# Sliding windows of 8 x 8: the early load on ScalarE's queue left out, and the eight last stores made into two

## The chip, the cores and the metric

The kernel runs on one core of a Trainium2 chip. The metric is the device time of one execution in microseconds. Before the change it is 190.47 us, the median of three runs (190.44 to 190.74).

## The reference

For every image, every window of 8 x 8 pixels with a stride of 4 is copied out, all 64 channels of it. There are 15 x 15 windows, so each input pixel is copied about four times: 16.78 MB come in, and 58.98 MB go out. Nothing is computed; the work is moving bytes.

```python
# x: [16, 64, 64, 64] float32, window_size 8, stride 4
for i in range(15):
    for j in range(15):
        result[:, i, j] = x[:, :, 4*i : 4*i + 8, 4*j : 4*j + 8]
# result: [16, 15, 15, 64, 8, 8]
```

## The kernel before

**The input in SBUF.** The whole input lies in one tile `L` of 128 partitions. A partition holds one image, one half of the channels (`ch`, 32 channels) and one band of 16 rows (`q`, four bands). Partition number: 64 x `ch` + 4 x image + `q`. So 32 neighbouring partitions (`QP`) are eight images (a block `y`, two of them) of one channel half, with all bands.

**The loads.** `load` (L56, issue at L58) brings one `ch`, `y` and `q`: eight partitions, every fourth. For each of the eight pairs of `y` and `q` there are three loads. SyncE's queue brings channels 4 to 31 of the first channel half (896 KB), GpSimd's queue channels 0 to 3 of it (128 KB) and the second channel half (1024 KB). Ahead of the loop ScalarE's queue issues one more load (L106): the first eight channels of band 0 of the second channel half, for all sixteen images, so 16 partitions and 512 KB. GpSimd's two loads of band 0 of the second half start behind these channels and are 768 KB each.

**The windows.** Four output tiles `G` of 128 partitions take turns (`tile_`). One partition of such a tile holds one whole window of one image, 64 channels x 8 x 8, which is 16 KB and one contiguous row of the output. `part` (L181) fills a tile for one `y`, in four blocks of 32 partitions by two channel halves; `unit` fills a tile for all images, with copies on ScalarE (L148) and shuffles on VectorE (L151, L158, and L162 for ScalarE's share). Windows that cross from one band to the next take their lower rows from the next partition (L151). Each filled tile is written by one indirect DMA from GpSimd (`scatter`, L128), which looks up the output row of every partition; 29 of these go out in all. A tile is filled again once its scatter has completed. All scatters stand in GpSimd's queue behind the loads.

**The last column.** Windows in column j = 14 that lie in one band, for the first two row positions (`s` = 0 and 1), have tiles of their own (L218 to L230). Only 64 partitions (32 to 95) of the tile are filled: two blocks of 32 partitions (`y`) by two channel halves (`ch`), `ch` 0 on ScalarE and `ch` 1 on VectorE, so two blocks for each engine. Four plain stores of 16 rows each follow, one for each band `q`; those of `s` = 0 go out on SyncE's queue, those of `s` = 1 in turn on SyncE's and ScalarE's.

```python
for s in range(2):
    g = tile_()
    ...
    for q in range(HQ):
        free((nc.sync, nc.scalar)[s * q % 2].dma_start(out=o_q[q * NSLOT + s, j], ...))
```

What sets the order: each engine and each queue works in the order of the program, with waits on the data and on the tiles. GpSimd's queue uses eight completion semaphores in turn, so its ninth load waits for its first.

Of the kernel before, what the change touches and what calls it, by code (L numbers as in the profile page):

```python
# [10 lines left out]
def kernel(  # L11
# [7 lines left out]
    nc = tc.nc  # L19
    P = nc.NUM_PARTITIONS  # L20

    B, C, H, W = x.shape
    Bo, NH, NW, Co, WSo, WSo2 = out.shape
    WS = int(window_size)
    ST = int(stride)
# [5 lines left out]
    CH = 2  # L31
    HQ = P // (B * CH)
    CL = C // CH
    RB = H // HQ
    NSLOT = RB // ST
    NWIN = NH * NW
    CFREE = C * WS * WS
    HP = P // CH
    YB = 8
    NY = B // YB  # L40
    QP = YB * HQ
# [7 lines left out]
    L = lpool.tile([P, CL, RB, W], f32)  # L49
# [6 lines left out]
    def load(eng, ch, y, q, c0, c1):  # L56
        p0 = ch * HP + y * QP + q
        eng.dma_start(out=L[p0 : p0 + QP - HQ + 1 : HQ, c0:c1, :, :], in_=x_v[ch, y, q, :, c0:c1, :])  # L58
# [41 lines left out]
    mul(th, tc_, NW)  # L100
    tt(idx_lo, idx_lo, th, ALU.add)


    EC = 8
    x_b = x.rearrange("b (ch cl) (hq r) w -> ch hq b cl (r w)", ch=CH, hq=HQ)
    nc.scalar.dma_start(out=L[HP : HP + (B - 1) * HQ + 1 : HQ, 0:EC, :, :], in_=x_b[1, 0, :, 0:EC, :])  # L106

    for y in range(NY):
        for q in range(HQ):
            hw = y * HQ + q < HWP  # L110
            if hw:
                load(nc.sync, 0, y, q, SMALL, CL)
            load(nc.gpsimd, 0, y, q, 0, SMALL if hw else CL)
            load(nc.gpsimd, 1, y, q, EC if q == 0 else 0, CL)

    o_v = out.rearrange("b i j c r w -> (b i j) (c r w)")
    nxt = [min(p + 1, 31) for p in range(32)]
# [3 lines left out]
    o_q = out.rearrange("b i j c r w -> i j b (c r w)")  # L121

    def free(st):
        tc.declare_no_dep(st.ins, group="stores", reason="each store writes rows of its own")
        tc.add_to_no_dep_group("stores", st.ins)
# [27 lines left out]
    act, dve = nc.scalar.copy, nc.vector.tensor_copy  # L153
# [15 lines left out]
    def tile_():  # L169
        nonlocal at  # L170
        at += 1
        return G[(at - 1) % NG]
# [43 lines left out]


    j = NW - 1  # L218
    tile_()
    for s in range(2):  # L220
        g = tile_()
        cols = slice(j * ST, j * ST + WS)
        for y in range(NY):
            d = slice(QP + y * QP, QP + (y + 1) * QP)
            for ch, copy in enumerate((act, dve)):
                f = slice(ch * HP + y * QP, ch * HP + (y + 1) * QP)
                copy(out=g[d, ch * CL : (ch + 1) * CL, :, :], in_=L[f, :, s * ST : s * ST + WS, cols])  # L227
        g_q = g.rearrange("p c r w -> p (c r w)")
        for q in range(HQ):
            free((nc.sync, nc.scalar)[s * q % 2].dma_start(out=o_q[q * NSLOT + s, j], in_=g_q[QP + q : QP + q + (B - 1) * HQ + 1 : HQ]))  # L230


# [33 lines left out]
```

## Time and profile before

| What | Before |
|---|---|
| Median of three runs | 190.47 us |
| The profiled execution | 190.74 us |
| Its span | 189.0 us |
| VectorE busy | 142.5 us (75%) |
| ScalarE busy | 139.2 us (74%) |
| GpSimd busy | 46.9 us (25%) |
| DMA, mean over the span | 401 GB/s, 11044 packets |
| GpSimd's queue (q0) | 65.81 MB, 84.0% of the 16 engines' span |
| SyncE's queue (q1) | 8.91 MB, 12.0% |
| ScalarE's queue (q10) | 1.05 MB, 1.8% |

The profile is of one execution, which took 190.74 us; its span, from the first to the last record, is 189.0 us. A line of the 40 slices gives the busy share in tenths, a slice being 4.7 us long. A share of DMA is the mean over the 16 engines. It can stand a little above 1, because packets overlap. The names in the queue lines: q0 "software_dynamic" is what GpSimd issues, q1 what SyncE issues, q10 what ScalarE issues.

### The profile page before, as it was taken

How to read it: one execution, taken by the hardware profiler on the slowest of the kernel's cores; microseconds unless marked ns; L12 is line 12 of the kernel's file. 1: busy time of each engine (PE TensorE's matmuls, PEld its weight loads, DVE VectorE, ACT ScalarE, POOL GpSimd, SP SyncE). 2: the span in 40 equal slices, each digit the busy share in tenths (PEclk: the TensorE clock that was granted, in tenths of full speed). 3: DMA queues.
4: the chain of work that ended last, by engine and by line, in shares of the span. 5: the costliest groups of instructions: out<-in, count | busy, mean ns of one | idle time of the engine just before them, and what ended most of it. 6: DMA issues, size and time to landing. Idle time of an engine off the chain costs nothing.

```text
span 189.0 us, 557 instructions
## 1 busy us (share of the span) xinstructions
DVE 142.5 (75%) x200; ACT 139.2 (74%) x89; POOL 46.9 (25%) x50
## 2 busy tenths in 40 slices
DVE  4000009999697979799989999999999999997410
ACT  0000009998699999988889999999999999974740
POOL 7321212207217170522220222222222222223000
DMA  4999999999999999999999999999999999999993
GB/s 118 308 409 397 402 401 397 397 403 394 427 434 420 435 434 416 434 434 413 437 437 408 439 430 420 423 437 416 427 413 434 428 409 430 406 437 378 427 389 153
DMA packets 11044, 75.81 MB, mean 401 GB/s; under 512 B 3344, under 2 KB 3344, under 8 KB 7440
## 3 DMA queue, kind: packets, MB, share of 16 engines
q0 software_dynamic: 8784, 65.81, 84.0%
q1 hardware_dynamic: 2048, 8.91, 12.0%
q10 hardware_dynamic: 208, 1.05, 1.8%
q14 instruction: 4, 0.03, 0.0%
HBM read 16.78 MB, written 62.91 MB: 422 GB/s over the span
## 4 chain that ended last, share of the span: by engine, by line
DMA 66%; DVE 18%; issue 6%; ACT 3%; POOL 2%; DVEq 0%; ACTq 0%; PEldq 0%
DMA out_dram<-G,idx_hi 24%; DMA L<-in_x_dram 23%; DMA out_dram<-G,idx 13%; DVE G L158 10%; DMA out_dram<-G,idx_y 7%; DVE G L151 5%; DVE G L181 3%; ACT G L227 2%; POOL L L58 2%; ACT G L148 1%; DVE G L148 0%; DVEq L181 0%; POOL pi L69 0%; DVEq L158 0%; PEldq L261 0%
## 5 line engine op out<-in xcount | busy, mean ns | idle before, releaser
L148 ACT COPY G<-L 64x2048 f32<-64x2048 f32 x46 | 87.2, 1896 | 5.5 <-DMA out_dram<-G,idx 2.3
L181 DVE COPY G<-L 32x2048 f32<-32x2048 f32 x30 | 36.6, 1221 | 29.3 <-DMA L<-in_x_dram 26.7
L158 DVE STREAM_SHUFFLE G<-L 64x1024 f32<-64x1024 f32 (+3 forms) x40 | 55.7, 1392 | 1.3
L151 DVE STREAM_SHUFFLE G<-L 64x1024 f32<-64x1024 f32 x30 | 38.5, 1282 | 0.0
L181 ACT COPY G<-L 32x2048 f32<-32x2048 f32 x18 | 33.9, 1896 | 2.9 <-DMA L<-in_x_dram 2.3
L181 ACT ACT_TABLE_LOAD x1 | 1.3, 1283 | 28.3 <-DMA L<-in_x_dram 28.3
L58 POOL DMA_DIRECT2D L<-in_x_dram x16 | 10.9, 691 | 23.0 <-DMA L<-in_x_dram 22.5
L128 POOL DMA_INDIRECT out_dram<-G,idx_y x6 | 10.0, 1664 | 25.5 <-DVE G L181 24.5
L128 POOL DMA_INDIRECT out_dram<-G,idx x8 | 11.3, 1412 | 19.9 <-DVE G L158 6.5
L128 POOL DMA_INDIRECT out_dram<-G,idx_hi x8 | 7.7, 963 | 30.7 <-DVE G L151 23.1
L128 POOL DMA_INDIRECT out_dram<-G,idx_lo x7 | 6.7, 961 | 27.5 <-DVE G L151 19.1
L227 ACT COPY G<-L 32x2048 f32<-32x2048 f32 x4 | 7.6, 1896 | 5.1 <-DMA out_dram<-G,idx_lo 4.0
L162 ACT COPY G<-L 64x256 f32<-64x256 f32 (+1 forms) x20 | 9.1, 456 | 0.5
L227 DVE COPY G<-L 32x2048 f32<-32x2048 f32 x4 | 4.9, 1219 | 3.5 <-DMA out_dram<-G,idx_hi 2.4
L148 DVE COPY G<-L 64x2048 f32<-64x2048 f32 x6 | 7.3, 1222 | 0.2
L158 DVE LOAD_MASK_SELECT G<-L x40 | 0.4, 9 | 2.1 <-DMA out_dram<-G,idx_y 1.2
L72 DVE TENSOR_SCALAR tb<-pi 128x1 int32<-128x1 int32 x1 | 0.2, 153 | 1.0 <-POOL pi L69 1.0
L78 DVE TENSOR_TENSOR th<-tc,tq 128x1 int32<-128x1 int32 x2 | 0.3, 156 | 0.0
L75 DVE TENSOR_SCALAR th<-tc 128x1 int32<-128x1 int32 x2 | 0.3, 154 | 0.0
L69 POOL IOTA pi<- 128x1 int32 x1 | 0.1, 124 | 0.4 <-PEq L261 0.4
L151 DVE LOAD_MASK_SELECT G<-L x30 | 0.2, 7 | 0.0
L78 DVE CUSTOM_DVE_ANT_0 idx_lo<-tb,th 128x2 uint16<-128x2 uint16 x1 | 0.2, 159 | 0.0
(18 smaller groups left out, 2.6 us busy)
## 6 DMA issues: line engine op xcount, KB each, us to landing
L<-in_x_dram SPq DMA_DIRECT2D x8, 896.0 KB
L<-in_x_dram POOLq DMA_DIRECT2D x6, 1024.0 KB, 21.6
L<-in_x_dram POOLq DMA_DIRECT2D x2, 768.0 KB, 18.3
out_dram<-G SPq DMA_DIRECT2D x6, 256.0 KB
L<-in_x_dram POOLq DMA_DIRECT2D x8, 128.0 KB, 21.6
L<-in_x_dram ACTq DMA_DIRECT2D x1, 512.0 KB
out_dram<-G ACTq DMA_DIRECT2D x2, 256.0 KB
out_dram<-G,idx POOLq DMA_INDIRECT x8, 12.3
```

What stands on the lines that cost most here:

```text
L58: eng.dma_start(out=L[p0 : p0 + QP - HQ + 1 : HQ, c0:c1, :, :], in_=x_v[ch, y, q, :, c0:c1, :])
L69: nc.gpsimd.iota(pi[:, :], pattern=[[0, 1]], base=0, channel_multiplier=1)
L72: nc.vector.tensor_scalar(out=d[:, :], in0=pi[:, :], scalar1=shift, scalar2=mask, op0=ALU.logical_shift_right, op1=ALU.bitwise_and)
L75: nc.vector.tensor_scalar(out=d[:, :], in0=a[:, :], scalar1=float(m), scalar2=None, op0=ALU.mult)
L78: nc.vector.tensor_tensor(out=d[:, :], in0=a[:, :], in1=b[:, :], op=op)
L128: st = nc.gpsimd.indirect_dma_start(out=o_v, out_offset=bass.IndirectOffsetOnAxis(ap=ix[:, 0:1], axis=0), in_=g.rearrange("p c r w -> p (c ...
L148: copy(out=g[d, cs, :, :], in_=L[f, :, s * ST : s * ST + WS, cols])
L151: nc.vector.stream_shuffle(out=g[d, cs, ST:WS, :], in_=L[f, :, 0:ST, cols], mask=nxt)
L158: nc.vector.stream_shuffle(out=out, in_=in_, mask=same)
L162: act(out=out[:, 0:k], in_=in_[:, 0:k])
L181: (act if (2 * d + ch) % 3 == 0 else dve)(out=g[d * QP : (d + 1) * QP, ch * CL : (ch + 1) * CL, :, :], in_=L[f : f + QP, :, s * ST : s * S ...
L227: copy(out=g[d, ch * CL : (ch + 1) * CL, :, :], in_=L[f, :, s * ST : s * ST + WS, cols])
```

## The change

Two edits. First, the early load on ScalarE's queue is gone, and GpSimd's two loads of band 0 of the second channel half bring all 32 channels. Second, the last two tiles are filled in another way, and each is stored by one transfer of 64 rows: the tile of `s` = 0 from SyncE's queue, that of `s` = 1 from ScalarE's. Of the four blocks of a tile, ScalarE fills the first (`y` 0, `ch` 0) and half the channels of another (`y` 1, `ch` 0). VectorE fills the two of `ch` 1 and the other half. The output rows are named in the order of the partitions, image by image and then band by band.

```diff
-    EC = 8
-    x_b = x.rearrange("b (ch cl) (hq r) w -> ch hq b cl (r w)", ch=CH, hq=HQ)
-    nc.scalar.dma_start(out=L[HP : HP + (B - 1) * HQ + 1 : HQ, 0:EC, :, :], in_=x_b[1, 0, :, 0:EC, :])
-
     for y in range(NY):
         for q in range(HQ):
             hw = y * HQ + q < HWP
             if hw:
                 load(nc.sync, 0, y, q, SMALL, CL)
             load(nc.gpsimd, 0, y, q, 0, SMALL if hw else CL)
-            load(nc.gpsimd, 1, y, q, EC if q == 0 else 0, CL)
+            load(nc.gpsimd, 1, y, q, 0, CL)
...
     j = NW - 1
+    half_c = CL // 2
     tile_()
     for s in range(2):
         g = tile_()
         cols = slice(j * ST, j * ST + WS)
-        for y in range(NY):
+        for y, ch, c0, c1, copy in (
+            (0, 0, 0, CL, act),
+            (0, 1, 0, CL, dve),
+            (1, 0, 0, half_c, act),
+            (1, 1, 0, CL, dve),
+            (1, 0, half_c, CL, dve),
+        ):
             d = slice(QP + y * QP, QP + (y + 1) * QP)
-            for ch, copy in enumerate((act, dve)):
-                f = slice(ch * HP + y * QP, ch * HP + (y + 1) * QP)
-                copy(out=g[d, ch * CL : (ch + 1) * CL, :, :], in_=L[f, :, s * ST : s * ST + WS, cols])
-        g_q = g.rearrange("p c r w -> p (c r w)")
-        for q in range(HQ):
-            free((nc.sync, nc.scalar)[s * q % 2].dma_start(out=o_q[q * NSLOT + s, j], in_=g_q[QP + q : QP + q + (B - 1) * HQ + 1 : HQ]))
+            f = slice(ch * HP + y * QP, ch * HP + (y + 1) * QP)
+            copy(
+                out=g[d, ch * CL + c0 : ch * CL + c1, :, :],
+                in_=L[f, c0:c1, s * ST : s * ST + WS, cols],
+            )
+        g_q = g.rearrange("p c r w -> p (c r w)")[QP : QP + B * HQ]
+        free((nc.sync, nc.scalar)[s].dma_start(out=o_q[s::NSLOT, j].rearrange("q b f -> b q f"), in_=g_q))
```

## Prediction

> **What bounds the kernel now.** I read the 40 slices of the page first, then the busy time by stretches, then the DMA queues in short windows at the start, then the timeline of the end. The slices say which resource is full:
>
> ```profile
> span 189.0 us, 557 instructions
> ...
> DMA  4999999999999999999999999999999999999993
> GB/s 118 308 409 397 402 401 397 397 403 394 427 434 420 435 434 416 434 434 413 437 437 408 439 430 420 423 437 416 427 413 434 428 409 430 406 437 378 427 389 153
> ```
>
> The sixteen DMA engines are busy in every slice but the first and the last. The bytes are given (16.78 MB read, 62.91 MB written), and neither changes. So time can be won or lost only where the engines stand idle, or where one of them has more to do than another. The stretches show where that is:
>
> ```profile
> core 0: us, DVE busy (x) ACT busy (x) POOL busy (x), PEclk, DMA share, GB/s
> 2.20:4.14 1.94, 1.27 (x10) 0.00 (x0) 1.94 (x5) 1.00 0.90 228
> 4.14:5.00 0.86, 0.00 (x0) 0.00 (x0) 0.86 (x2) 1.00 0.85 176
> 5.00:6.25 1.25, 0.00 (x0) 0.00 (x0) 1.25 (x3) 1.00 0.85 233
> 6.25:10.00 3.75, 0.00 (x0) 0.00 (x0) 0.77 (x2) 1.00 1.00 359
> 10.00:28.00 18.00, 0.00 (x0) 0.00 (x0) 3.03 (x5) 1.00 1.04 402
> 50.00:97.60 47.60, 42.94 (x49) 44.36 (x27) 14.33 (x9) 1.00 1.01 428
> 97.60:172.00 74.40, 72.97 (x112) 67.98 (x48) 15.40 (x16) 1.00 1.01 424
> 181.40:186.50 5.10, 0.00 (x0) 0.01 (x1) 0.00 (x0) 1.00 0.82 341
> ```
>
> From 10 us to 172 us the share is 1.0 and the rate 400 to 428 GB/s. Slow are the start (2.2 to 6.25 us, about 220 GB/s) and the last stores (341 GB/s). Both edits sit exactly there. The queues of the start, packets and MB in the windows 0 to 4.14 us and 4.5 to 5 us:
>
> ```profile
> q10 hardware_dynamic: 109, 0.44, 42.3%
> ...
> q1 hardware_dynamic: 12, 0.05, 46.4%
> q10 hardware_dynamic: 13, 0.02, 17.0%
> q0 software_dynamic: 35, 0.00, 7.0%
> ```
>
> q10 is ScalarE's queue (the early load that goes), q1 SyncE's, q0 GpSimd's. Until 4.14 us only q10 moves, although SyncE issued its first load at 0.74 us, in the same instant, and GpSimd ended its first issue at 2.23 us. The single packet records show why: on each engine the first packet of another queue starts about 6 ns after q10's last one (4.138, then 4.144; 4.216, then 4.221; 5.273, then 5.279). The other two queues were ready and stood behind the early load.
>
> **Two halves of the engines.** The trace's completion records show one thing more, on which my sum rests. A GpSimd load completes in two groups of eight engines. Its 1024 KB loads complete in the first group at 15.4, 20.5 and 25.7 us, so 5.1 us apart, which is 206 GB/s: eight engines at a 4 KB packet per 159 ns each, without a pause. In the other group the same loads complete at 19.0, 25.9 and 32.6 us, at the pace of SyncE's loads. So GpSimd's loads of the second channel half run on eight engines (I call them upper), SyncE's loads and GpSimd's 128 KB loads on the other eight (lower). The 16-row load of ScalarE runs on all sixteen. KB before: lower 8 x 896 + 8 x 128 + 256 = 8448, upper 6 x 1024 + 2 x 768 + 256 = 7936. The upper half ends its loads at 45.0 to 46.5 us, the lower at 47.2 to 48.9. That lead stays to the end: the first scatter completes at 50.6 us (upper) and 52.7 (lower), the last but one at 174.5 and 176.9. The lower half is full from its first packet to its last and sets the end; its lag is 2.1 to 2.4 us.
>
> **Edit 1, the early load.** After it both halves have 8192 KB.
> Lower half: the early load's eight packets per engine go, and SyncE's first load takes their place at 2.2 us instead of 4.14. That is 8 x 0.159 = 1.27 us less. It could be up to 1.9, since SyncE's first packets, 0.32 us each, are slow too and would be slow while GpSimd's are not there. I take -1.3.
> Upper half: sixteen more packets per engine in GpSimd's queue (two loads of 1024 KB for two of 768), 16 x 0.159 = +2.54 us. Against that, GpSimd's queue need not wait for q10. Today its first packets are at 4.51 us, its steady flow at about 6.25. How early it would be ready, no row shows. One bound is 4.5 us, nothing won. The other is from the first scatter: its issue ended at 44.69 us, and its first packet ran at 45.32 on engines that had run out of loads, so 0.63 us after; 2.23 + 0.63 = 2.9 us, 1.6 us won. I take 1.35, near that row, since the 6 ns hand-over says that the queue was waiting, and allow a quarter of a microsecond for a cold start. Net for the upper half +1.2 us, bounds +0.9 and +2.5. It has 2.1 to 2.4 us of lead, so measured against the old lower half it is at -0.9 to -1.2, with the bounds -1.5 and +0.4.
> The later of the two halves sets the end: the upper, at about -1.1 us.
> The Trainium skill ("DMA: Bandwidth & Descriptors", "Issuing engines are not separate DMA queues") says that transfers issued from ScalarE, SyncE and GpSimd run on the same sixteen DMA engines and interleave. The 6 ns rows show the same engines, but no interleaving while the early load's eight packets last. If they did interleave, the early load would hold nobody up: the upper half would be out only its 256 KB more, +1.27 us, and the sum would be near the same, about -1.0.
> A rule of the same page speaks against this edit ("Latency and other measured facts"): a transfer from SyncE or ScalarE has its first byte after about 0.6 us, one from GpSimd after about 1 us. By it the bytes move to the queue that starts later, and an estimate from that page would put GpSimd's first packet at 3.2 us, the upper half at +1.3, the sum at -1.0. No run here shows a GpSimd queue starting alone.
>
> **What hangs on the loads.** GpSimd's loads 9 to 16 each wait for the completion of the one eight before; behind them in its queue stand the scatters. On the lower engines a second-half load shows only 4-byte packets, 32 per engine for a 1024 KB load, which take turns with SyncE's 4 KB packets (5.4 us per load); the larger first load has 8 more, +1.3 us, against its queue's earlier start, -1.35. So the first copies stay at 28.4 us within about 1.3. If they are 1.3 late, that is covered twice: VectorE stands idle from 47.05 to 48.97 us for the last loads, and the first scatter (43.3 us) has its first packets when the upper half ends its loads, now at about 46. Without that cover it costs at most the same 1.3 us. SyncE's queue loses nothing, and ScalarE has nothing else to do at 0.74 us.
>
> **Edit 2, the two last stores.** Today:
>
> ```profile
> 172.70 3.81 ACT L227 COPY G<-L 32x2048 f32<-32x2048 f32 x2 [3.99 <-DMA out_dram<-G,idx_lo]
> 172.75 2.45 DVE L227 COPY G<-L 32x2048 f32<-32x2048 f32 x2 [1.00 <-DMA out_dram<-G,idx_lo]
> 176.54 7.58 SPq L230 DMA_DIRECT2D out_dram<-G  x6
> 177.59 3.81 ACT L227 COPY G<-L 32x2048 f32<-32x2048 f32 x2 [1.07 <-DMA out_dram<-G,idx_hi]
> ...
> 181.44 2.19 ACTq L230 DMA_DIRECT2D out_dram<-G  x2
> ```
>
> ScalarE is last, with 2 x 1.90 us. Now it has one and a half blocks: its copies of 512 and 2048 elements take 0.62 and 1.90 us, so 1024 take 1.04, together 2.94. VectorE has 2 x 1.22 + about 0.65 = 3.1. The stores are ready 0.7 us sooner, and one issue stands for four. ScalarE's issue also waits for VectorE, but nothing is queued behind it.
> What is that worth? The engines lose 0.18 x 5.1 = 0.9 us in the last stretch, and that is the upper bound. But it is mostly the upper half that idles: the lower half completes 16 rows of 16 KB between 177.2 and 187.2 us, 0.625 us each, where a row's packet takes 0.615. The half that is late has its rows queued whenever the stores come, so I take -0.1 us, bounds 0 and -0.9. Each engine moves four rows per store either way.
>
> **Sum.** -1.1 - 0.1 = -1.2 us. The profiled execution took 190.74 us, of which 189.0 are the span; it would be 189.5. The median of before is 0.27 lower, so the forecast is 189.3 us; its own range, from the bounds -0.6 and -1.7 of the two halves, is 188.8 to 189.9.
>
> **Rivals.**
> No change: GpSimd's queue is ready by itself only shortly before 4.5 us. Then the upper half takes +2.3 to +2.5, its lead is gone, and it ends where the lower did: 190.2 to 190.7. For it: it is the first issue of that queue, and after its first packets the first data took another 1.2 us. Against it: the 6 ns.
> Slower: the upper half becomes the late one. It moved 7680 KB in 39.1 us (6.1 to 45.2), 196 KB per us, so 512 KB more are 2.6 us; against the smaller lead of 2.1 that is +0.5, 191.0 us. It decides once GpSimd's first packets come later than about 4.4 us; the place is the end of the upper half's loads, after 47.5 us. For it: whole queues have started late here. Against it: nothing but q10 ran on those engines then.
> More: both halves near their best bound and the idle time of the last stretch won as well, -1.6 - 0.7: 188.2 us. For it: stores ready sooner, halves level. Against: the full lower half.
> The edit doesn't do what it says: the 64-row store runs on fewer engines, as the 8-row loads do. On four it is 16 rows of 0.615 us on each instead of four, +7.4 us, 197.9. Against it: 16-row transfers here run on all sixteen, and its outer dimension is the same 16 images.
>
> **How the numbers follow.** Forecast 0.55, more 0.15, no change 0.15, slower 0.12, store on fewer engines 0.03. A measurement of this kernel can tell 0.2% (0.38 us) from no change. Faster by over that: 0.55 + 0.15 = 0.70; within: 0.15; slower: 0.15. The range goes from the "more" case to well into the slower one: 188.1 to 190.9 us; outside it are the fewer engines and the outer ends of the others.
>
> **What would show it.** Right: SyncE's queue moves at about 2.2 us and GpSimd's by about 3.2 (now 4.14 and 4.51); the windows 2.2 to 6.25 us carry SyncE's and GpSimd's packets side by side; the last load lands before 48 us (now 48.9), and every later scatter is a microsecond sooner; the last fills take about 3.1 us. Wrong: GpSimd's first packets at 4.5 us again, or the wait for the last load at 49 us as now; or, in the last stretch, a share of DMA far below 0.82.

## The result, and the profile after

The changed kernel takes 191.91 us (median of six runs, 191.58 to 192.09) against 190.55 for the kernel before in the same comparison: ratio 1.0068, 95% interval 1.0055 to 1.0081. It is 1.4 us slower; the forecast was 1.2 us faster. The profiled execution has a span of 190.1 us (189.0 before). The 40 slices of the changed kernel:

```profile
span 190.1 us, 551 instructions
...
DMA  2999999999999999999999999999999999999993
GB/s 81 311 404 402 402 399 396 402 399 399 431 431 424 419 438 424 414 417 431 431 396 440 415 414 431 424 424 407 441 410 414 433 414 421 421 427 400 441 383 141
```

As in the prediction, the upper and the lower half are the two groups of eight DMA engines, and a row is one packet of 16 KB, one window of the output; a scatter gives each engine eight rows, or fewer where it leaves rows out.

The engines are about as full as before. The same stretches as in the prediction (busy time of the three engines, TensorE clock, share of DMA, GB/s), for the changed kernel:

```profile
core 0: us, DVE busy (x) ACT busy (x) POOL busy (x), PEclk, DMA share, GB/s
2.20:4.14 1.94, 1.26 (x10) 0.00 (x0) 1.94 (x5) 1.00 0.49 144
4.14:5.00 0.86, 0.00 (x0) 0.00 (x0) 0.86 (x2) 1.00 0.48 186
5.00:6.25 1.25, 0.00 (x0) 0.00 (x0) 1.25 (x3) 1.00 0.94 288
6.25:10.00 3.75, 0.00 (x0) 0.00 (x0) 0.80 (x2) 1.00 1.02 340
10.00:28.00 18.00, 0.00 (x0) 0.00 (x0) 2.41 (x4) 1.00 1.03 400
50.00:97.60 47.60, 42.58 (x50) 43.76 (x28) 14.65 (x11) 1.00 1.01 425
97.60:172.00 74.40, 73.00 (x111) 67.78 (x48) 15.39 (x16) 1.00 1.00 420
181.40:186.50 5.10, 0.93 (x2) 0.72 (x1) 0.00 (x0) 1.00 0.90 379
```

Two things are to be seen. At the start the share in 2.2 to 5 us has fallen from 0.85 to 0.90 down to 0.49, so half of the engines stand idle there. And where nothing was edited, from 50 to 172 us, the rate is 425 and 420 GB/s instead of 428 and 424, at a share that is the same within 0.01: the engines are as busy, but their packets take longer. That is 0.7 and 0.9 per cent of 47.6 and 74.4 us, together about 1.0 us, nearly as much as the whole change that the prediction reckoned with (1.2 us).

The queues of the changed kernel in the window 0 to 4.14 us, packets and MB:

```profile
q1 hardware_dynamic: 68, 0.28, 22.5%
q0 software_dynamic: 40, 0.00, 0.4%
```

SyncE's loads (q1) now move here, as was forecast. Of GpSimd's (q0) there are forty packets, but no bytes to speak of: they are the 4-byte ones of its first load.

From the completion records, the time at which the last engine of the lower half was done, in each profiled execution:

| Stage (lower half) | Before, us | After, us | Difference of the stage |
|---|---|---|---|
| First scatter complete | 53.65 | 52.82 | -0.83 |
| Last scatter but one complete | 177.51 | 179.08 | +2.40 |
| Last store complete | 187.61 | 188.84 | -0.34 |
| End of the span | 188.96 | 190.13 | -0.07 |

The loads gave roughly what they were to give. The last stretch is shorter too, but that isn't the new stores alone: from the last scatter but one to the last completion it takes 10.1 us in the kernel before and 9.8 both with the store edit alone and with the load edit alone, which has the old stores. The 2.4 us in between made the change a loss. By the first of the eight engines instead of the last, the first two differences are -0.2 and +1.9 us. The upper half lost nothing in between: 123.9 us from its first scatter to its last but one before, 123.4 after.

### The profile page after: what moved, and what is told of

Same layout as the page of the kernel before. It is cut to its first block, busy times and chain, and to the rows that moved or that the text cites. A ratio compares the mean times of both kernels' runs of the same rounds, so it can differ in the third digit from the quotient of the medians.

```text
span 190.1 us, 551 instructions
## 1 busy us (share of the span) xinstructions
DVE 144.0 (76%) x202; ACT 137.5 (72%) x89; POOL 46.6 (24%) x50
## 3 DMA queue, kind: packets, MB, share of 16 engines
HBM read 16.78 MB, written 62.91 MB: 419 GB/s over the span
## 4 chain that ended last, share of the span: by engine, by line
DMA 48%; DVE 38%; issue 7%; POOL 2%; DVEq 1%; PEldq 0%
DMA L<-in_x_dram 21%; DVE G L153 18%; DVE G L146 14%; DMA out_dram<-G,idx_hi 13%; DMA out_dram<-G,idx 8%; DMA out_dram<-G,idx_y 6%; DVE G L176 5%; POOL L L58 2%; DVE G L228 1%; DVEq L264 1%; DVE G L143 0%; DVEq L176 0%; POOL pi L69 0%; DVEq L153 0%; DVEq L228 0%
## 5 line engine op out<-in xcount | busy, mean ns | idle before, releaser
L176 DVE COPY G<-L 32x2048 f32<-32x2048 f32 x30 | 36.6, 1221 | 29.0 <-DMA L<-in_x_dram 26.1
L176 ACT COPY G<-L 32x2048 f32<-32x2048 f32 x18 | 33.9, 1896 | 1.2 <-DMA out_dram<-G,idx_y 0.8
L123 POOL DMA_INDIRECT out_dram<-G,idx_y x6 | 10.9, 1810 | 24.0 <-DVE G L176 14.4
L123 POOL DMA_INDIRECT out_dram<-G,idx x8 | 10.0, 1246 | 20.1 <-ACT G L157 10.6
L228 ACT COPY G<-L 32x2048 f32<-32x2048 f32 (+1 forms) x4 | 5.9, 1470 | 5.7 <-DMA out_dram<-G,idx_lo 3.6
L228 DVE COPY G<-L 32x2048 f32<-32x2048 f32 (+1 forms) x6 | 6.2, 1041 | 4.3 <-DMA out_dram<-G,idx_lo 2.4
```

Of the source, the lines that this page charges most:

```text
L123: st = nc.gpsimd.indirect_dma_start(out=o_v, out_offset=bass.IndirectOffsetOnAxis(ap=ix[:, 0:1], axis=0), in_=g.rearrange("p c r w -> p (c ...
L176: (act if (2 * d + ch) % 3 == 0 else dve)(out=g[d * QP : (d + 1) * QP, ch * CL : (ch + 1) * CL, :, :], in_=L[f : f + QP, :, s * ST : s * S ...
L228: copy(out=g[d, ch * CL + c0 : ch * CL + c1, :, :], in_=L[f, c0:c1, s * ST : s * ST + WS, cols],)
```

## The experiments

I tested theories of where that middle stretch lost its time: S, that the two halves of the engines slow each other when they end the loads together; Q, and later N, that it is the missing early load itself; L, that the lower half is slow once it trails the upper by too little; and T, that it is the stores. All runs were timed in five rounds beside the kernel before.

**Each edit alone.** `tail_only`: the kernel before with the new last part (the second half of the diff).

> The kernel before with edit 2 alone (the two 64-row stores). Theory S (step): the change lost its time between 60 and 172 us, because its two halves of the DMA engines end the loads together instead of 2.3 us apart and then slow each other; the stores gained a little. Theory Q (queue): the time was lost because the early load is gone and GpSimd's queue carries its bytes, whatever the two halves do. Theory T (tail): the 64-row stores cost the time. S and Q expect 190.0 to 190.5 us, T about 191.8.

Measured: 190.22 us against 190.46, ratio 0.9987 (0.9978 to 0.9995). This speaks against T: with the early load in place the new stores win 0.24 us.

`loads_only`: the first half of the diff, with the old stores.

> Edit 1 alone (no early load), with the eight old stores. S and Q expect 191.9 to 192.5 us and 425 and 420 GB/s in the windows 50 to 97.6 and 97.6 to 172 us, as in the changed kernel (428 and 424 before). T expects 189.6 to 190.0.

Measured: 191.52 us, ratio 1.0050 (1.0037 to 1.0063), which is 0.4 us below the range of S and Q and far from that of T. So 1.1 us of the loss comes with the load edit alone; the rest is taken up below, at `after_again`. In the windows of the prediction, 50 to 97.6 and 97.6 to 172 us, the store edit alone has 428 and 424 GB/s, as before, the load edit alone 423 and 420. Windows 60 to 110 and 110 to 160 us of the kernel before:

```profile
60.00:110.00 50.00, 46.16 (x63) 46.39 (x30) 14.13 (x11) 1.00 1.01 427
110.00:160.00 50.00, 49.30 (x75) 47.55 (x36) 10.59 (x11) 1.00 1.01 425
```

and of the load edit alone:

```profile
60.00:110.00 50.00, 45.69 (x63) 45.22 (x29) 11.69 (x11) 1.00 1.01 422
110.00:160.00 50.00, 49.13 (x75) 46.00 (x34) 10.59 (x11) 1.00 1.01 421
```

The lower rate comes with the load edit, 10 us and more after the last load has landed. With the store edit alone these two windows have 427 and 423 GB/s, so a difference of 2 GB/s in the second of them tells nothing.

**The old lead given back, without the early load.**

```diff
-            load(nc.gpsimd, 1, y, q, 0, CL)
+            SH = 8 if (y, q) == (NY - 1, HQ - 1) else 0
+            if SH:
+                load(nc.sync, 1, y, q, 0, SH)
+            load(nc.gpsimd, 1, y, q, SH, CL)
```

> The changed kernel, with the first eight channels of the last second-half load (256 KB) moved from GpSimd's queue to the end of SyncE's, which puts them on the lower half of the engines. The lower half has more work than in the changed kernel and ends its loads about 1.3 us later (48.1 to about 49.4), the upper earlier, so the old lead of 2 us is there again. S expects the rates of before (428 and 424 GB/s) and 190.2 to 190.9 us, faster than the changed kernel though its loads end later. Q expects the low rates to stay, and 192.5 to 193.2.

Measured: 191.67 us, ratio 1.0056 (1.0043 to 1.0069), between the two theories. Its windows:

```profile
60.00:110.00 50.00, 46.34 (x62) 46.87 (x30) 13.92 (x11) 1.00 1.01 427
110.00:160.00 50.00, 49.27 (x77) 46.10 (x34) 10.19 (x11) 1.00 1.01 422
```

The rate is that of before up to 110 us, though there is no early load: against Q. It costs a later end of the loads (the lower half has its first scatter complete at 54.5 us, 1.7 later than in the changed kernel), and yet the kernel is no slower than the changed one. The halves move as many bytes here as in the kernel before (8448 KB on the lower, 7936 on the upper), but the last load lands at 49.9 us instead of 48.9: that is most of the 1.1 us that this kernel loses. The last scatter but one is 124.7 us after the first on the lower half, against 126.1 in the changed kernel and 124.2 before (first of the eight engines), so three quarters of the loss in the middle are gone.

**The halves levelled, with the early load kept.** In the last group of loads:

```diff
+            mv = 7 if (y, q) == (NY - 1, HQ - 1) else 0
-            if hw:
-                load(nc.sync, 0, y, q, SMALL, CL)
-            load(nc.gpsimd, 0, y, q, 0, SMALL if hw else CL)
+            load(nc.sync, 0, y, q, SMALL + mv, CL)
+            if mv:
+                load(nc.gpsimd, 0, y, q, 0, 2)
+                load(nc.gpsimd, 0, y, q, SMALL, SMALL + mv)
+                load(nc.gpsimd, 0, y, q, 2, SMALL)
+            else:
+                load(nc.gpsimd, 0, y, q, 0, SMALL)
```

> The kernel before with its early load and edit 2, but in the last group of loads seven channels of the first half (224 KB) move from SyncE's queue to a GpSimd load that falls on the upper half. That levels the halves: the lower ends its loads about 1.1 us sooner, the upper later, lead near zero. S expects the slow rate (packets of 16 KB about 624 ns instead of 616 in 75 to 97 us) and 190.9 to 191.8 us. Q expects the rate of before and about 189.2 us.

Measured: 191.56 us, ratio 1.0055 (1.0042 to 1.0067). The time is what S expected, but for another reason, and S is wrong:

```profile
60.00:110.00 50.00, 45.97 (x63) 45.85 (x30) 12.91 (x10) 1.00 1.01 430
110.00:160.00 50.00, 49.30 (x75) 46.20 (x34) 10.59 (x11) 1.00 1.00 423
```

The halves are 0.2 us apart here after the loads, and up to 97 us they run faster than in any other kernel: a row of 16 KB takes 612.8 ns (mean, 75 to 97 us), where it takes 615.7 before and 624.2 in the changed kernel. Running in step does not by itself slow them. After about 105 us the lower half is slow all the same. Over 60 to 172 us the mean row is no longer than before (617.8 against 618.5 ns): this kernel loses by its late loads and by the distance between its halves, 3.0 us at the last scatter but one (2.4 before). The end of the loads, which was to come 1.1 us sooner, came only 0.2 sooner on the lower half. The last GpSimd load was issued only at 39.0 us instead of 33.9, since two loads more wait for completions, and the upper half stood without work: from 40 to 42 us the engines moved 195 GB/s, against 395 with the store edit alone. So Q's number says nothing here.

**More and less of the early load.** The number of channels in it (`EC`), with the new stores:

```diff
-    EC = 8
+    EC = 4        # and 16
```

> Edit 2 alone, with an early load of four channels instead of eight. It has half the early load's effect on the loads: the lower half ends them 0.6 us sooner than with eight, the upper 0.6 later, so the lead at the first scatter is about 1 us instead of 2.1. Theory L (lead): the lower half writes a scatter of eight rows in 4.85 us as long as it trails the upper by more than about 1.2 us, and in 5.0 us once it has come nearer; then the slow pace begins before 90 us here (at about 127 us with eight channels, at 67 without the load), and the time is 190.7 to 191.4 us. Theory N (no load): the slow pace comes only without an early load; then the pace is as with eight, and the time is 189.6 to 190.0 us (190.2 with eight).

> Edit 2 alone, with an early load of sixteen channels (1 MB). The lower half ends its loads 1.3 us later than with eight channels, the lead at the first scatter is about 4 us. L expects the pace of 4.85 us to hold past 150 us, which pays back 0.7 to 1.4 us of the later loads: 190.2 to 190.9 us. N expects the same pace as with eight, so the full 1.3 us more: 191.4 to 191.7.

Measured: four channels 191.16 us, ratio 1.0036 (1.0023 to 1.0049); sixteen 192.07 us, 1.0085 (1.0071 to 1.0099). Four is what L expected, and 1.2 us above what N did, although the loads ended sooner than with eight. With sixteen the pace did what L said, but the time was 1.2 us above its range (and 0.4 above N's): the larger load put off the first scatter of the lower half by 2.1 us (52.9 to 55.0) and not by 1.3. The completion records of all these kernels show the pace. Slow means that a scatter with eight rows for each lower engine completes 4.97 us or more after the one before, by the first engine of the half; fast is about 4.85.

| Kernel | Early channels | First scatter complete, upper and lower | Lower half slow from | Rows of 16 KB, 60 to 172 us, mean ns |
|---|---|---|---|---|
| loads_only | 0 | 52.1, 52.3 | 62 us | 624.2 |
| changed kernel | 0 | 52.2, 52.6 | 72 us | 623.9 |
| ec4 | 4 | 51.3, 52.2 | 82 us | 622.2 |
| level8 | 8 | 52.9, 53.2 | 111 us | 617.8 |
| split8 | 0 | 52.0, 53.7 | 120 us | 619.7 |
| before | 8 | 50.6, 52.7 | 127 us | 618.5 |
| tail_only | 8 | 50.7, 52.9 | 127 us | 618.8 |
| ec16 | 16 | 51.6, 55.0 | 178 us | 617.3 |

In all of these kernels but the levelled one, the smaller the head start of the upper half, the sooner the lower half falls from 4.85 to 5.0 us for eight rows. This holds with the early load and without it (split8). The levelled kernel is against it: a head start of 0.2 us, and fast up to 105 us. The times in the table are also rough. The changed kernel fell at 67 us in a second execution (`after_again`, below), and `flip0` (below), whose scatters are the same up to 90 us, at 82 us. So without the early load the fall comes anywhere from 62 to 82 us, and four channels can't be told from none by it.

**Two rows fewer for the half that ends last.**

```diff
-            turn = crossed % 2
+            turn = (crossed + 1) % 2
```

> Edit 2 alone, with the turns of the units that cross bands swapped: eight scatters with idx_lo and seven with idx_hi instead of seven and eight. The lower half leaves out two rows per engine with each idx_lo, the upper with each idx_hi, so the lower half has 224 rows per engine instead of 226, the upper 226. If the lower half alone sets the end, this is worth up to 2 x 0.61 = 1.2 us: 189.0 to 189.6. Under L the lower half comes nearer to the upper by the same rows, falls to the slow pace earlier and loses most of it again: 189.8 to 190.3. Under N 189.0.

> The swapped turns together with an early load of sixteen channels: more lead, and fewer rows for the half that trails. L expects the fast pace to hold and the rows to be saved in full: 189.2 to 189.8 us. N expects 1.3 us more than the swapped turns with eight channels: 190.3 to 190.6.

Measured: 189.42 us with eight channels, ratio 0.9948 (0.9934 to 0.9962); 190.95 with sixteen, 1.0031 (1.0020 to 1.0041). With eight it beats both kernels. The swap is worth 0.8 us at eight channels (from 190.22) and 1.1 at sixteen (from 192.07); both are near the 1.2 us of two rows. L missed at eight: from 95 us on the lower half trails the upper by only 0.2 to 0.7 us after every crossing scatter in which it leaves out its rows, and stays fast until 135 us. So a fixed distance of 1.2 us is not what switches the pace. With sixteen, 190.95 is above the ranges of L and of N, by the same late loads as above.

The same swap in the changed kernel:

> The changed kernel with the turns of the crossing units swapped, so that the lower half writes 224 rows per engine instead of 226 and the upper 226 instead of 224. If in the changed kernel the lower half is the late one and in its slow pace (5.0 us for eight rows, 0.625 each), this is worth 2 x 0.62 = 1.2 us, so 190.2 to 190.8 us, as it was with the early load (1.0 us there). If the upper half set the end of the changed kernel, as the prediction had it, the swap costs up to 1.2 us instead: 192.5 to 193.1.

Measured: 190.52 us, ratio 1.0004 (0.9995 to 1.0014), against 191.96 for the changed kernel on the same chip. The swap wins 1.4 us, so in the changed kernel too it is the lower half that ends last. The completion records say the same: the last scatter but one completes at 175.8 us on the upper half and at 179.1 on the lower.

The changed kernel once more, to see whether the two edits add up:

> The changed kernel as it is, beside the swapped one on one chip: 191.4 to 192.1 us. It tells whether edit 2, which won 0.13% with the early load in place, also wins without it, where edit 1 alone took 191.52 us: if the two edits add up, 191.3.

Measured: 191.96 us, ratio 1.0081 (1.0067 to 1.0095). The edits don't add up: the stores win 0.24 us with the early load and, beside 191.52 for the load edit alone, seem to cost 0.4 without it (ratio 1.0081 against 1.0050; the first comparison gave 1.0068, which is not clear of 1.0050). In the profiles the last packet ends at 188.6 us in the load edit alone and at 188.5 in the changed kernel, so the stores end no later. What differs is the time from the last completion to the end of the span, 0.9 us against 1.3 (1.2 with the store edit alone). It does not go with the form of the stores, since the kernel before, with the old ones, has 1.4. Why that is so was not tried.

**What stays open.** What throws the lower half from one pace to the other is not settled. The packet records show only when the slow packets come (here all rows over 660 ns). Between 60 and 172 us the changed kernel has 173 rows over 660 ns, and 148 of them start 2.0 to 3.0 us after GpSimd begins to issue a scatter, mostly five to eight at a time; of all its rows, 21% start in that band. The kernel before has 36, of which 29 in that band. So they go with the arrival of a new scatter. But in the levelled kernel scatters arrive in the same way up to 93 us, and nearly every row takes about 611 ns there. No run moved the issues alone to test it.

## Why the prediction was wrong

**The step that failed** is that only the start and the end would move: that after its loads each half goes on at its own pace, so that "the later of the two halves sets the end" with an unchanged middle. Of the upper half the prediction said "That lead stays to the end", and it put the change of the middle at nothing. The runs show a middle that is not fixed: 2.4 us more on the lower half from the first scatter to the last but one, since its scatters of eight rows fell from 4.85 to 5.0 us apart at 72 us instead of 127. That makes up the distance from the forecast 1.2 us faster to the measured 1.4 us slower, but for 0.2. Why the fall comes sooner stays open. I had the tell-tale in the completion records before: the lower half's scatters of eight rows 4.85 us apart up to 122 us and 5.0 after, and the upper's about 4.94 all along. I read one pace out of the mean.

**The upper half as the late one** was wrong as well. The swap of the crossing turns shows that the lower half ends last, and the upper half's lead of 2.1 to 2.4 us was not idle margin that could be used up for nothing: in all kernels of the table but the levelled one, a smaller lead went with an earlier fall of the lower half's pace. Levelling the bytes (8192 KB for each half) bought nothing here.

**SyncE's start** was right: its first packets run at 2.34 us (4.14 before), and its first load completes from 9.0 us on instead of 10.3, the -1.3 of the sum. The lower half as a whole completed its loads 0.8 us sooner.

**GpSimd's start** was mis-sized. Its first packets run at 2.86 us, as the row of the first scatter had it (2.9). But these are the 4-byte packets of its first load. Its first data on the upper half, from the second load, came at 5.10 us (5.04 before) though that issue had ended at 2.95, and the steady flow at about 5.9 instead of 6.25. So the queue's earlier start was worth 0.4 us and not 1.35; I let the first packet stand for the data. The whole upper half ended its loads at 47.7 us instead of 46.5 by its last engine, the +1.2 of the forecast, but at 47.2 instead of 45.0 by its first, +2.2 us, as the late data would have it. The Trainium skill's figure of about 1 us to the first byte of a transfer from GpSimd ("DMA: Bandwidth & Descriptors", "Latency and other measured facts") does not fit the second load either, whose data took 2.1 us from the end of its issue. The slower rival named this place: GpSimd's packets after 4.4 us. Its price, +0.5 us by a late upper half, was not what happened: the upper half ended its loads at 47.2 to 47.7 us and was still ahead.

**The loads' end and the copies** went nearly as reckoned. The last load landed at 48.1 us instead of 48.9 (-0.8 against -1.1). The first copies started 1.4 us later (29.8 us), the first scatter was issued 1.35 later (44.7), and the cover held: the first scatter completed on the lower half no later than before.

**The stores** were right in their own terms: fills of 3.0 and 3.2 us (2.94 and 3.1 forecast), and a gain of 0.24 us with the early load in place (0.1 forecast). Without it no gain was seen. The end of the changed kernel in order of time:

```profile
174.14 2.96 ACT L228 COPY G<-L 32x2048 f32<-32x2048 f32 x2 [3.57 <-DMA out_dram<-G,idx_lo]
174.18 3.15 DVE L228 COPY G<-L 32x2048 f32<-32x2048 f32 x3 [2.40 <-DMA out_dram<-G,idx_lo]
177.41 0.65 SPq L233 DMA_DIRECT2D out_dram<-G  x1
...
182.45 0.64 ACTq L233 DMA_DIRECT2D out_dram<-G  x1
```

One issue of 0.65 us stands where the six old issues on SyncE's queue took 7.6 us. The fills start 1.4 us later than before, since the scatters that free their tiles are late by then. That a 64-row store would run on fewer engines is out: the stores' rows complete on all sixteen.

**Two smaller points.** The forecast's own range, -0.6 to -1.7 us, was said to come from the bounds of the two halves, but the upper half's own bounds ran up to +0.4 there; the range was too narrow for its own working (the wider one, 188.1 to 190.9 us, takes that bound in). And the 62.91 MB written, from the page, count the rows that scatters leave out: the packet records have 3600 rows of 16 KB, 58.98 MB. Nothing in the sum rests on that number.

## What to carry to other kernels

In a kernel that is full of DMA from end to end, a share of 1.0 does not say that the rate is fixed: look at how long the packets take, in several stretches and for each group of engines, before you put a stretch down as unchanged. When a load is moved to another queue, reckon with its first data and not with the queue's first packet. And where one group of engines ended last, giving it fewer rows (189.42 us) beat every attempt here to start it sooner.

## What the runs showed of the hardware

Not expected: a row of 16 KB has more than one price under the same load. In the levelled kernel up to 93 us it was 611 ns for nearly every row on both halves. In the changed kernel it was up to 700 ns and more, mostly for five to eight rows at once, near the arrival of a scatter, and 624 ns in the mean over 112 us. Which of these a half of the engines ran at went with the load edit, tens of microseconds after the loads had ended; what sets it stays open.

Nor was it expected that GpSimd's second load would have its first data 2.1 us after its issue had ended, on engines that had nothing else to do, while 0.62 us passed from the end of the first issue to the first of its 4-byte packets.
